# Forty products of a zero block ahead of TensorE's first transposes, an early load of ScalarE's tables, and a new order of the first loads

## The chip, the cores and the metric

The kernel runs on one core of a Trainium2 chip. The metric is the device time of one execution in microseconds (us), as the median of several runs. One more execution was taken by the hardware profiler; its trace gives the rows that are quoted.

## What is computed

Two layers of a transformer trunk for 512 sample tokens and 128 prompt tokens of width 2048, which share all weights. Everything is float32. Cut to what matters:

```python
for layer in range(2):
    sh_p, sc_p, gt_p = modulation(c_ctx, ada_w[layer], ada_b[layer])   # silu(cond) @ ada_w + ada_b
    sh_s, sc_s, gt_s = modulation(c, ada_w[layer], ada_b[layer])       # ada_w[layer]: 2048 x 6144
    hp = rms_norm(xp, norm_g[layer]) * (1.0 + sc_p) + sh_p
    hs = rms_norm(xs, norm_g[layer]) * (1.0 + sc_s) + sh_s
    if layer % 2 == 0:
        out_p, (kc, vc) = even_mixer(hp, *w)      # h @ ev_w_in, banded attention and gated conv, @ ev_w_out
        out_s, _ = even_mixer(hs, *w, ctx=..., rope=rope)
    else:
        out_p, (ckc, cvc, dkc, dvc) = odd_mixer(hp, *w)
        out_s, _ = odd_mixer(hs, *w, ctx=..., rope=rope)
    xp = xp + gt_p * out_p
    xs = xs + gt_s * out_s
```

## The kernel before, in words

Activations stand transposed: a tile `h{k}` holds 128 of the 2048 features (k from 0 to 15) for all 640 tokens, as a high and a low part (`hi`, `lo`). A weight block of 128 x 128 is split in the same way (`wh` by ScalarE, `wl` by VectorE, lines 227 and 228), and a product is three matmuls (`wh` by `hi`, `wh` by `lo`, `wl` by `hi`) for each half of 320 tokens, in the banks `pa`, `pb` or the two halves of `Sp`. The engines' order is made by a scheduler when the program is built; each engine then takes its instructions strictly in that order.

The change touches the **start**. It runs so:

1. SP, ScalarE's queue and GpSimd's queue load the identity, the conditions `c` and `c_ctx` and other short rows (into `rows_a` and `rows_b`, lines 104 to 115) and the tokens, in ten pieces of 512 KB (`xb`, line 101; five blocks of 128 tokens, two halves each).
2. ScalarE and VectorE make silu of the conditions (lines 122 and 123); TensorE transposes the result, and VectorE writes it to `sT` (lines 126 and 127).
3. `x_block` (lines 945 to 960) transposes each token block on TensorE in four groups of four (line 951); VectorE copies three of the groups and ScalarE one (line 952). A group is held in one of two `psT` banks. ScalarE also squares the block (line 956).
4. `ada_on_pe` (lines 173 to 190) multiplies `sT` by tiles of `ada_w` (line 180, "T<-ada,sT" in the profile), which gives scale and shift of a few features at a time. SP loads these tiles by `ada_load` (line 169), 1 MB each, into four buffers that are taken in turn. From unit 1 on, a round of four tiles gives two features: two tiles the scale, two the shift.
5. `lead_units` (lines 331 to 387) works through the features: unit 0 takes features 0 and 1 one after the other (lines 351 to 353), each further unit takes two features (lines 263 to 265). In every unit eight column blocks of the weights are multiplied; for six of them the result is added to a `sum` tile (lines 383 and 385). While unit u runs, the modulation of unit u + 1 is worked out (`ahead`, which calls `ada_group`), and its weights are loaded (`load_two`, line 328, tag `raw`, 4 buffers of 256 KB, two loads each).

Before the change `rows_a`, `rows_b` and `th` are tiles of the tag `raw` too, so three of the four weight buffers are first taken by short rows. Each load counts on one of eight landing semaphores, which the loads of SP's and ScalarE's queue use in turn (DMAHW0 to DMAHW7 in the rows further down): a load of these queues waits until the eighth load before it has landed.

Of the kernel before, what the change touches and what calls it, by code (L numbers as in the profile page):

```python
# [11 lines left out]
F32 = mybir.dt.float32  # L12
F32R = mybir.dt.float32r
BF16 = mybir.dt.bfloat16
AF = mybir.ActivationFunctionType
# [5 lines left out]
P = 128  # L21
# [23 lines left out]
RAW_AHEAD = 5  # L45
SPLIT_AHEAD = 3
FILL0 = 1.68


@with_exitstack  # L50
def trunk_kernel(ctx: ExitStack, tc: tile.TileContext, I: dict, O: dict):
    nc = tc.nc
    V, A, PE, G = nc.vector, nc.scalar, nc.tensor, nc.gpsimd
# [3 lines left out]
    wpool = ctx.enter_context(tc.tile_pool(name="w", bufs=W_BUFS))  # L57
# [6 lines left out]
    def psT():  # L64
        return pT.tile([P, 512], F32, tag="T", name="T")

    def load_rows(dst, name):
        nc.sync.dma_start(dst, I[name][0].partition_broadcast(P))
# [23 lines left out]
    vec = const.tile([P, 160], F32, name="vec")  # L92
    open_pool("start")
    sp = pre = pools["cur"]
    rows_a = wpool.tile([P, P], F32, tag="raw", name="rows_a")
    def x_load(b):
        src = I["x_sample"][0, b * P:(b + 1) * P, :] if b < 4 else I["x_prompt"][0]
        ts = []
        for g in range(2):
            ts.append(hpool.tile([P, 1024], F32, tag=f"h{15 - 2 * b - g}", name="xb"))  # L100
            (nc.scalar if b < 2 else nc.sync).dma_start(ts[g], src[:, g * 1024:(g + 1) * 1024])
        return ts

    nc.sync.dma_start(ident, I["k_ident"])
# [2 lines left out]
    nc.gpsimd.dma_start(rows_a[32:64, :], I["norm_g"].rearrange("l (k p) -> (l k) p", p=P))  # L107
    nc.gpsimd.dma_start(rows_a[64:112, :], I["ada_b"][0].rearrange("(k p) -> k p", p=P))
    xs = [x_load(b) for b in range(5)]
    rows_b = wpool.tile([P, P], F32, tag="raw", name="rows_b")  # L110
    nc.gpsimd.dma_start(rows_b[0:48, :], I["ada_b"][1].rearrange("(k p) -> k p", p=P))
    nc.gpsimd.dma_start(rows_b[48:72, :], I["b_conv"][0].rearrange("t (k p) -> (t k) p", p=P))
    nc.gpsimd.dma_start(rows_b[72:74, :], I["c_out_norm"].rearrange("b (k p) -> (b k) p", p=P))
    for i, n in enumerate(("a_q_norm", "c_q_norm", "d_q_norm")):
        nc.gpsimd.dma_start(rows_b[74 + i:75 + i, :], I[n])

    ada_t = [pre.tile([P, 2048], F32, name=f"ada{i}") for i in range(4)]
    ada_sb = pre.tile([P, 512], F32, name="ada_sb")
    h_t = [pre.tile([P, NT], F32, name=f"ht{i}") for i in range(2)]

    th = wpool.tile([32, P], F32, tag="raw", name="th")
    A.activation(th, rows_a[0:32, :], AF.Tanh, scale=0.5)
    V.scalar_tensor_tensor(out=rows_a[0:32, :], in0=th, scalar=1.0, in1=rows_a[0:32, :],
                           op0=ALU.add, op1=ALU.mult)
# [40 lines left out]
    def ada_load(l, cb, kt, b0, n):  # L165
        m = 16 // n
        w = ada_t[0].rearrange("p (k n) -> p k n", k=m)
        ada_t.append(ada_t.pop(0))
        nc.sync.dma_start(w, I["ada_w"][l, kt * P:(kt + m) * P, cb * 512 + b0 * P:cb * 512 + (b0 + n) * P]
                          .rearrange("(k p) n -> p k n", p=P))  # L170
        return w

    def ada_on_pe(l, cb, b0, n, ws=None):

        acc, m, wd = psT(), 16 // n, n * P
        for kt in range(KT):
            if kt % m == 0:
                w = ws[kt // m] if ws else ada_load(l, cb, kt, b0, n)
            g = kt % 4
            PE.matmul(acc[32 * g:32 * g + 32, 0:wd], sT[:, kt, :], w[:, kt % m, :],  # L180
                      start=(kt < 4), stop=(kt >= KT - 4), tile_position=(0, 32 * g))
        sb = ada_sb
        A.copy(sb[:, 0:wd], acc[:, 0:wd])
        tr = psT()
        for j in range(n):
            PE.transpose(tr[:, j * P:(j + 1) * P], sb[:, j * P:(j + 1) * P], ident)
        red = small.tile([P, n, 2], F32, tag="red", name="red", bufs=2)
        V.tensor_reduce(red, tr[:, 0:wd].rearrange("p (b g c) -> p b c g", b=n, g=4)[:, :, 0:2, :], axis=AX.X,
                        op=ALU.add)
        add_bias(l, cb, red, b0, n)  # L190
        ada_done(l, cb, b0, n)
# [703 lines left out]
    band = const.tile([P, 3, P], BF16, name="band")  # L895
# [4 lines left out]
    gain_rows = const.tile([P, 3, P], F32, name="gain_rows")  # L900
    gains = {n: vec[:, 154 + i:155 + i] for i, n in enumerate(("a_q_norm", "c_q_norm", "d_q_norm"))}
    gains.update({n: gain_rows[:, i, :] for i, n in enumerate(("a_k_norm", "c_k_norm", "d_k_norm"))})
    sink = const.tile([P, 8], F32, name="sink")
# [65 lines left out]
    def ada_group(g, js):  # L969
        for cb in (4 + g, g):  # L970
            ada_on_pe(0, cb, js[0], js[1] - js[0])
        if g == 3 and js[1] == 4:
            for i, n in enumerate(("a_k_norm", "c_k_norm", "d_k_norm")):
                load_rows(gain_rows[:, i, :], n)
            nc.sync.dma_start(band, I["k_band"])
            load_rows(sink, "a_sink")

    def first_loads(cols):

        scale = [ada_load(0, 4, 0, 0, 1)]  # L980
        raws = [load_two(I["ev_w_in"][0], cols[0:2], 0)]
        shift = [ada_load(0, 0, 0, 0, 1)]
        raws += [load_two(I["ev_w_in"][0], cols[i:i + 2], 0) for i in (2, 4, 6)]
        x_block(0, xs[0])
        vec_rows(0, 80, rows_a, 32)
        for b in range(1, 5):
            x_block(b, xs[b])
        last_act[0] = put[0]
        ada_on_pe(0, 4, 0, 1, scale)
        x_rows((0, 1, 2, 3))  # L990
        x_rows((4,))
        vec_rows(80, 77, rows_b, 0)
        ada_on_pe(0, 0, 0, 1, shift)
        return raws
# [143 lines left out]
    for i in range(5, 8):  # L1138
        b_tiles(i)

    u0, c0, b0, h0, g0, g1 = jobs[4:10]
    jobs[0:10] = [u0, c0, jobs[0], jobs[1], g0, jobs[2], jobs[3], g1, b0, h0]
    raws = first_loads([jobs[n][0] for n in (0, 2, 1, 3, 4, 5, 6, 7)])
    run_tiles(jobs, I["ev_w_in"][0], h0_maker, fill0, FILL0, ada_group, trans=TRANS, grace=GRACE, cut=((0, 2), (2, 4)),
              summed=keep, led=even_start, freed=ada_start, first=raws)
    drain(prep)
# [643 lines left out]
```

## Time and profile before

| | |
|---|---|
| median of 3 runs | 2289.78 us (2287.35 to 2291.44) |
| the profiled execution, own time | 2292.61 us |
| its span, first to last instruction | 2290.8 us |
| TensorE busy (matmul) | 2257.0 us, 99% |
| VectorE busy | 1603.5 us, 70% |
| ScalarE busy | 1087.0 us, 47% |
| chain that ended last, share of TensorE | 87% |
| chain that ended last, share of DMA | 3% |

The times in the profile's rows count from the first instruction of the span; 1.8 us of the execution's own time lie around the span. In a row of the timeline stand the start, the time taken, the engine, the line and the instruction; in square brackets how long the engine sat idle before it and what ended that. "SPq" and "ACTq" are instructions that issue a DMA: their duration holds the wait for a free place. One product of float32 operands is two rows of the trace on TensorE ("x10" for five products), a transpose is one. Busy times of TensorE overlap, so a group's cost is read from start to start.

### The profile page before, as it was taken

The page shows a single profiled execution, that of the slowest core. Times are in us where ns is not written, and L with a number is a line of the kernel's source. Part 1 is how long each engine was busy: PE and PEld are TensorE (multiplying, and loading weights), DVE is VectorE, ACT ScalarE, POOL GpSimd, SP SyncE. Part 2 cuts the span into 40 slices and gives each one's busy share as a digit, 9 for nine tenths or more (in the row PEclk, how much of TensorE's full clock was granted, in tenths as well). Part 3 has the DMA queues.
Part 4 walks back from the last instruction along what each step waited for, and adds up shares of the span by engine and source line. Part 5 has one row for each costly group of instructions (what it writes and reads, how often), then busy time and mean ns, then how long its engine had stood idle before and what let it go on. Part 6 is the DMA issues. An engine that isn't in the chain of part 4 may idle for free.

```text
span 2290.8 us, 41085 instructions
## 1 busy us (share of the span) xinstructions
PE 2257.0 (99%) x15941; PEld 2178.5 (95%) x15941; DVE 1603.5 (70%) x2830; ACT 1087.0 (47%) x2281; POOL 162.6 (7%) x226
## 2 busy tenths in 40 slices
PE   7999999999999999999999999999999999999999
PEld 5889999999999999999999999999999999999999
DVE  5666969779779776787787666566566655557775
ACT  5224544244352222544464444465565676654443
POOL 1001000000000000000100001111111100000101
PEclk9999999999999999999999999999999999999999
DMA  9975555555538564854553333423213221238542
GB/s 322 318 224 182 172 155 171 182 153 169 183 107 255 171 190 135 275 168 147 163 157 106 116 118 115 142 61 104 86 56 102 71 65 58 65 109 271 167 137 62
DMA packets 385395, 344.20 MB, mean 150 GB/s; under 512 B 16418, under 2 KB 342528, under 8 KB 384688
## 3 DMA queue, kind: packets, MB, share of 16 engines
q1 hardware_dynamic: 370624, 296.66, 43.4%
q0 software_dynamic: 13856, 42.76, 5.4%
q8 instruction: 125, 2.05, 0.4%
q10 hardware_dynamic: 720, 2.16, 0.3%
q14 instruction: 70, 0.57, 0.1%
HBM read 301.93 MB, written 39.59 MB: 149 GB/s over the span
## 4 chain that ended last, share of the span: by engine, by line
PE 87%; DVE 5%; ACT 4%; DMA 3%; issue 2%; POOL 0%; SPq 0%; DVEq 0%; POOLq 0%; ACTq 0%
PE pq L597 7%; PE pq L596 7%; PE pq L595 7%; PE pa L263 6%; PE pa L264 6%; PE pa L265 6%; PE pb L264 6%; PE pb L263 5%; PE pb L265 5%; PE pb L278 2%; PE pb L277 2%; PE pa L277 2%; PE pb L279 2%; PE pa L279 2%; PE pa L278 2%; PE T L799 2%
## 5 line engine op out<-in xcount | busy, mean ns | idle before, releaser
L227 ACT ACTIVATE wh<-raw 128x512 fp32r<-128x512 f32 x418 | 263.3, 630 | 553.9 <-PE pb L264 388.0
L228 DVE TENSOR_TENSOR wl<-raw,wh 128x512 fp32r<-128x512 f32 x418 | 287.8, 689 | 200.4 <-ACT wh L227 176.8
L263 PE MATMUL pa<-h,wh 128*128 128x320 f32 x978 | 311.2, 319 | 2.4 <-ACT h L227 2.4
L264 PE MATMUL pa<-h,wh 128*128 128x320 f32 x978 | 306.0, 314 | 3.0 <-DVE h L228 2.2
L265 PE MATMUL pa<-h,wl 128*128 128x320 f32 x978 | 303.9, 311 | 0.0
L264 PE MATMUL pb<-h,wh 128*128 128x320 f32 x978 | 302.7, 310 | 0.0
L265 PE MATMUL pb<-h,wl 128*128 128x320 f32 x978 | 302.4, 309 | 0.0
L263 PE MATMUL pb<-h,wh 128*128 128x320 f32 x978 | 301.9, 309 | 0.0
L205 DVE SCALAR_TENSOR_TENSOR acc<-adaw,sT,acc 128x1024 f32<-128x1024 f32 x240 | 300.2, 1278 | 0.0
L595 PE MATMUL pq<-h,wh 128*128 128x320 f32 x672 | 209.2, 311 | 2.3 <-ACT wh L227 2.3
L597 PE MATMUL pq<-h,wl 128*128 128x320 f32 x672 | 208.4, 310 | 0.1
L596 PE MATMUL pq<-h,wh 128*128 128x320 f32 x672 | 208.1, 310 | 0.0
L263 PEld LDWEIGHTS pa<-h,wh 128*128 128x128 f32 x978 | 184.3, 189 | 16.0 <-issue 9.1
L264 PEld LDWEIGHTS pa<-h,wh 128*128 128x128 f32 x978 | 184.7, 189 | 10.5 <-DVE h L228 4.6
L265 PEld LDWEIGHTS pa<-h,wl 128*128 128x128 f32 x978 | 184.7, 189 | 0.4 <-issue 0.4
L264 PEld LDWEIGHTS pb<-h,wh 128*128 128x128 f32 x978 | 183.6, 188 | 1.0 <-issue 0.8
L263 PEld LDWEIGHTS pb<-h,wh 128*128 128x128 f32 x978 | 183.4, 188 | 0.5 <-DVE sum L385 0.4
L265 PEld LDWEIGHTS pb<-h,wl 128*128 128x128 f32 x978 | 183.6, 188 | 0.0
L597 PE MATMUL pq<-T,wl 128*128 128x320 f32 x504 | 155.1, 308 | 0.2 <-DVE wl L228 0.2
L596 PE MATMUL pq<-T,wh 128*128 128x320 f32 x504 | 155.3, 308 | 0.0
L595 PE MATMUL pq<-T,wh 128*128 128x320 f32 x504 | 155.0, 308 | 0.1
L277 PE MATMUL pa<-h,wh 128*128 128x320 f32 x448 | 146.0, 326 | 0.0
(463 smaller groups left out, 5414.1 us busy)
## 6 DMA issues: line engine op xcount, KB each, us to landing
adaw<-in_ada_w SPq DMA_DIRECT2D x128, 512.0 KB, 4.2
raw<-in_ev_w_in SPq DMA_DIRECT2D x176, 256.0 KB, 3.4
raw<-in_od_w_in SPq DMA_DIRECT2D x154, 256.0 KB, 2.9
ada<-in_ada_w SPq DMA_DIRECT2D x32, 1024.0 KB, 9.9
w<-in_od_w_in SPq DMA_DIRECT2D x27, 512.0 KB, 3.9
yd<-y POOLq DMA_DIRECT2D x32, 320.0 KB, 3.6
yin<-yd SPq DMA_DIRECT2D x32, 320.0 KB, 4.5
w<-yd SPq DMA_DIRECT2D x32, 320.0 KB, 4.5
```

The costliest lines, as they stand in the source:

```text
L205: V.scalar_tensor_tensor(out=acc[c], in0=w, scalar=sT[:, kt, c:c + 1], in1=acc[c], op0=ALU.mult, op1=ALU.add)
L227: A.activation(hi, x, AF.Copy)
L228: V.tensor_sub(lo, x, hi)
L263: PE.matmul(ps, wh[:, i, :], hi[:, sl], start=(j == js[0] if alone else (pos == 0 and j == 0)), stop=False)
L264: PE.matmul(ps, wh[:, i, :], lo[:, sl], start=False, stop=False)
L265: last_mm[0] = PE.matmul(ps, wl[:, i, :], hi[:, sl], start=False, stop=(j == js[1] - 1 if alone else (pos == 3 and j == 3)))
L277: PE.matmul(ps, wh[:, j, :], hi[:, sl], start=(qd == 0 and j == 0), stop=False)
L278: PE.matmul(ps, wh[:, j, :], lo[:, sl], start=False, stop=False)
L279: PE.matmul(ps, wl[:, j, :], hi[:, sl], start=False, stop=(qd == 3 and j == 3))
L595: PE.matmul(ps, wh[:, j, :], hi, start=(new and h == 0 and j == 0), stop=False, **kw)
L596: PE.matmul(ps, wh[:, j, :], lo, start=False, stop=False, **kw)
L597: PE.matmul(ps, wl[:, j, :], hi, start=False, stop=(h == 1 and j == 3), **kw)
```

## The change

- A tile `cold` of 128 x 128 is set to zero by VectorE; ScalarE takes the hyperbolic tangent of its first column, ahead of the other work of ScalarE.
- TensorE multiplies `cold` by itself 40 times, into a `psT` bank that nobody reads, ahead of its first transpose.
- The two halves of each sample block are loaded by two queues: the first half by ScalarE's queue, the second by SP's. Before, blocks 0 and 1 were ScalarE's and the others SP's. The prompt block stays with SP.
- `rows_a`, `rows_b` and `th` have places of their own and no longer take buffers of the tag `raw`.
- Four short loads at the end of the modulation are tied behind the last `ada_w` load.

```diff
+WARM = 40
...
     sp = pre = pools["cur"]
-    rows_a = wpool.tile([P, P], F32, tag="raw", name="rows_a")
+    cold = pre.tile([P, P], F32, name="cold")
+    V.memset(cold, 0.0)
+    A.activation(cold[:, 0:1], cold[:, 0:1], AF.Tanh)
+    rows_a = pre.tile([P, P], F32, name="rows_a")
     def x_load(b):
         src = I["x_sample"][0, b * P:(b + 1) * P, :] if b < 4 else I["x_prompt"][0]
         ts = []
         for g in range(2):
             ts.append(hpool.tile([P, 1024], F32, tag=f"h{15 - 2 * b - g}", name="xb"))
-            (nc.scalar if b < 2 else nc.sync).dma_start(ts[g], src[:, g * 1024:(g + 1) * 1024])
+            (nc.sync if b > 3 or g else nc.scalar).dma_start(ts[g], src[:, g * 1024:(g + 1) * 1024])
         return ts
...
-    rows_b = wpool.tile([P, P], F32, tag="raw", name="rows_b")
+    rows_b = pre.tile([P, P], F32, name="rows_b")
...
+    last_ada = [None]
...
+    warm = psT()
+    for _ in range(WARM):
+        PE.matmul(warm[:, 0:P], cold, cold, start=True, stop=True)
+
-    th = wpool.tile([32, P], F32, tag="raw", name="th")
+    th = pre.tile([32, P], F32, name="th")
...
-        nc.sync.dma_start(w, I["ada_w"][l, kt * P:(kt + m) * P, cb * 512 + b0 * P:cb * 512 + (b0 + n) * P]
+        last_ada[0] = nc.sync.dma_start(w, I["ada_w"][l, kt * P:(kt + m) * P, cb * 512 + b0 * P:cb * 512 + (b0 + n) * P]
...
         if g == 3 and js[1] == 4:
-            for i, n in enumerate(("a_k_norm", "c_k_norm", "d_k_norm")):
-                load_rows(gain_rows[:, i, :], n)
-            nc.sync.dma_start(band, I["k_band"])
-            load_rows(sink, "a_sink")
+            with tc.issue_after(last_ada[0].ins):
+                for i, n in enumerate(("a_k_norm", "c_k_norm", "d_k_norm")):
+                    load_rows(gain_rows[:, i, :], n)
+                nc.sync.dma_start(band, I["k_band"])
+                load_rows(sink, "a_sink")
```

The change adds ten lines, so line 180 of the kernel before is line 189 after it, lines 263 to 265 are 272 to 274, and lines 351 to 353 are 360 to 362. Since the scheduler orders the program anew, more moves than the diff shows. Three places matter.

**ScalarE's first instructions.** Before, then after ("cold" is the zero block, "xb" a token half, "th" the hyperbolic tangent of the conditions):

```order
L101 DMA xb<-in_x_sample 128x1024 x4
L122 ACT_TABLE_LOAD
L122 ACTIVATE th<-rows_a 32x128
L956 ACTIVATE sqj,s_224<-xb 128x1024 x2
L956 ACTIVATE sqj,s_260<-xb 128x1024 x2
L952 COPY xT_208<-T 128x4x128
```

```order
L105 DMA xb<-in_x_sample 128x1024
L98 ACT_TABLE_LOAD
L98 ACTIVATE cold<-cold 128x1
L105 DMA xb<-in_x_sample 128x1024 x3
L131 ACTIVATE th<-rows_a 32x128
L965 ACTIVATE sqj,s_268<-xb 128x1024 x2
```

The table load now stands ahead of the activation of the conditions, and three of the four loads on this queue stand behind it. On TensorE the row "L128 MATMUL T<-cold 128x128 x40" stands ahead of everything else.

**SP's queue**, from the last loads of unit 0 to the first tile of the modulation's next round. Before, then after, with the semaphores that each load waits for (`ada_120` to `ada_123` before and `ada_123` to `ada_126` after are the four buffers of `ada_w` tiles):

```order
L169 DMA ada_123<-in_ada_w 128x8x256 [waits DMAHW6_49,DMAHW4_49,PE_49]
L328 DMA raw<-in_ev_w_in 128x2x128 [waits DMASW5_49,DMASW6_49,DMASW4_49,DMASW7_49,DMASW3_49,DMASW2_49]
L328 DMA raw<-in_ev_w_in 128x2x128
L328 DMA raw<-in_ev_w_in 128x2x128 [waits DMAHW7_49,DVE_49]
L328 DMA raw<-in_ev_w_in 128x2x128 [waits DMAHW0_49]
L328 DMA raw<-in_ev_w_in 128x2x128 [waits DMAHW1_49,DVE_49]
L328 DMA raw<-in_ev_w_in 128x2x128 [waits DMAHW2_49]
L328 DMA raw<-in_ev_w_in 128x2x128 [waits DMAHW3_49,DVE_49]
L328 DMA raw<-in_ev_w_in 128x2x128 [waits DMAHW4_49]
L169 DMA ada_120<-in_ada_w 128x8x256 [waits DMAHW5_49,PE_49]
```

```order
L178 DMA ada_125<-in_ada_w 128x8x256 [waits DMAHW7_49,DMAHW4_49,PE_49]
L178 DMA ada_126<-in_ada_w 128x8x256 [waits DMAHW5_49,DMAHW0_49,PE_49]
L337 DMA raw<-in_ev_w_in 128x2x128 [waits DMAHW6_49]
L337 DMA raw<-in_ev_w_in 128x2x128 [waits DVE_49]
L337 DMA raw<-in_ev_w_in 128x2x128
L337 DMA raw<-in_ev_w_in 128x2x128 [waits DMAHW1_49,DVE_49]
L337 DMA raw<-in_ev_w_in 128x2x128 [waits DMAHW2_49]
L337 DMA raw<-in_ev_w_in 128x2x128 [waits DMAHW3_49,DVE_49]
L337 DMA raw<-in_ev_w_in 128x2x128 [waits DMAHW4_49]
L178 DMA ada_123<-in_ada_w 128x8x256 [waits DMAHW5_49,PE_49]
```

Between the last tile of one round and the first tile of the next, eight weight loads stood before and seven stand now; the eighth went ahead of the round's second tile. The place of that first tile in the queue is the same, and so is the set of loads ahead of it. The semaphore it waits for, DMAHW5, belongs to the first of the eight weight loads before, and to the last `ada_w` tile now.

**TensorE at the first product with that tile** (`ada_120` before, `ada_123` now). Before, then after ("h" with a high number are activations of unit 0's second feature or of unit 1):

```order
L263 MATMUL pb<-h_764,wh 128x320
L351 MATMUL pb<-h_609,wh 128x320
L352 MATMUL pb<-h_609,wh 128x320
L353 MATMUL pb<-h_609,wl 128x320
L180 MATMUL T<-ada_120,sT 32x256 x5
L351 MATMUL pa<-h_609,wh 128x320
L352 MATMUL pa<-h_609,wh 128x320
L353 MATMUL pa<-h_609,wl 128x320
L351 MATMUL pb<-h_609,wh 128x320
L352 MATMUL pb<-h_609,wh 128x320
L353 MATMUL pb<-h_609,wl 128x320
L180 MATMUL T<-ada_120,sT 32x256 x3
```

```order
L360 MATMUL pa<-h_653,wh 128x320
L361 MATMUL pa<-h_653,wh 128x320
L362 MATMUL pa<-h_653,wl 128x320
L189 MATMUL T<-ada_123,sT 32x256
L360 MATMUL pb<-h_653,wh 128x320
L361 MATMUL pb<-h_653,wh 128x320
L362 MATMUL pb<-h_653,wl 128x320
L189 MATMUL T<-ada_123,sT 32x256 x4
L360 MATMUL pa<-h_653,wh 128x320
L361 MATMUL pa<-h_653,wh 128x320
L362 MATMUL pa<-h_653,wl 128x320
L360 MATMUL pb<-h_653,wh 128x320
```

Counted from the start of the program, 98 matmuls of 320 tokens stand ahead of the tile's first product before, and 75 now. The 32 products of the round's four tiles stand in five runs before (5, 3, 8, 8 and 8 products) and in nine now (1, 4, 3, 1, 6, 1, 1, 7 and 8); the 32 of the following round stand in three runs before (16, 8 and 8) and in two now (16 and 16). From there on TensorE's order is the same up to small exchanges inside a unit, as is the order of the other engines.

## The prediction

> **What bounds the kernel now.** I read the page first (TensorE busy 99%, 87% of the chain of waits), then that chain by time, for the places where TensorE is not what sets the pace. Near the start, which is all that the change touches, it has these pieces (start, length, what):
>
> ```profile
> 1.67 5.06 DMA rows_a<-in_c_ctx
> 13.60 4.51 PE T L951 x20
> 18.88 0.67 PE T L951 x4
> 24.64 0.67 PE T L951 x4
> 26.08 1.12 PE T L180 x32
> 48.02 8.43 DMA ada<-in_ada_w
> 56.59 1.02 PE T L180 x10
> ```
>
> Until 6.7 us everything waits for a short row. Until 26.08 the token blocks are transposed. Then a chain of small steps leads into unit 0. At 48.02 an `ada_w` tile is issued that lands at 56.45, and TensorE stands still for it. The timeline has TensorE's side of that:
>
> ```profile
> 54.98 0.31 PE L351 MATMUL pb<-h,wh 128*128 128x320 f32 x1
> 56.59 1.02 PE L180 MATMUL T<-ada,sT 128*32 128x256 f32 x10 [1.01 <-DMA ada<-in_ada_w]
> 78.65 1.93 PE L180 MATMUL T<-ada,sT 128*32 128x256 f32 x32
> 97.89 1.86 PE T L180 x32
> ```
>
> So TensorE is released by a landing at 56.45. From there the windows show it busy throughout, and no later piece of the chain up to 190 us is a DMA. What comes after 56.6 us is TensorE's own work, so **the end is the landing of that tile plus the TensorE work that stands behind it**. The landing in turn is set by the DMA engines:
>
> ```profile
> 14.00:16.00 2.00, 2.00 (x11) 1.67 (x10) 1.10 (x3) 1.97 (x4) 0.57 (x1) 1.00 1.03 422
> 26.00:28.00 2.00, 1.53 (x36) 1.27 (x37) 0.81 (x3) 1.37 (x3) 0.00 (x0) 1.00 1.15 326
> 44.00:46.00 2.00, 2.00 (x20) 1.07 (x17) 0.81 (x2) 0.41 (x1) 0.00 (x0) 1.00 1.11 344
> 48.00:50.00 2.00, 2.00 (x27) 1.39 (x20) 1.74 (x4) 0.86 (x2) 0.00 (x0) 1.00 0.71 184
> 70.00:72.00 2.00, 2.00 (x15) 1.85 (x14) 1.97 (x4) 1.83 (x4) 0.00 (x0) 1.00 1.06 353
> ```
>
> The last three columns are granted clock, DMA share and GB/s. The share is over 1 from 8 us to 48 us; only around 49 us it drops. The loads ahead of the tile are as fast as they can be, whatever the engines do.
>
> **The change part by part.**
>
> *The forty products.* The nearest rows are five products of the same form at full speed, and transposes, slow and fast:
>
> ```profile
> 0.95 0.48 DVE L91 MEMSET sT<- 128x512 f32 x1
> 27.71 1.29 PE L966 MATMUL T<-ident,rx 128*128 128x128 f32 x10
> L951 PE MATMUL T<-ident,xb 128*128 128x128 f32 x11 | 2.8, 431 | 0.3 <-DVE vec L132 0.3
> L951 PE MATMUL T<-ident,xb 128*128 128x128 f32 x13 | 2.2, 285 | 0.2
> ```
>
> The last two are the windows 14 to 16 and 18 to 20 us: a transpose goes from 431 to 285 ns, and the chain's 20 from 13.60 give 4.51 / 20 = 0.226 us each while slow. The granted-clock column says 1.00 in both, so I go by the durations. A product is two rows, 2 x 1.29 / 10 = 0.26 us fast with the tail, some 0.23 in a long run, and twice a slow transpose, 0.45, slow. The zero block is ready after VectorE's 1.43 and about 0.2 for a quarter of that memset; I start at 1.8. Forty products end between 1.8 + 40 x 0.23 = 11.0 (never slow) and 1.8 + 40 x 0.45 = 19.8 (never fast). In the trace TensorE became fast near 17.6, 8.8 us after its first work at 8.77 and 4.0 us after its last pause at 13.60. With 4.0 us slow (9 products, 31 fast) the end is 12.9; with 8.8 us (20 and 20) it is 15.2. The products run without pause, so I take 13.5.
>
> The Trainium skill, "TensorE: Matmul & The Clock Gate" (The HAM clock gate), has the default clock halved and released after one busy window of about 3.4 us, which runs free of the kernel; by it the release comes 3.4 to 6.8 us after the start and the products end at an estimated 12.7 to 14.4. The trace agrees with its halving: 0.226 us a transpose against 0.11 us a row fast.
>
> *The transposes behind them.* The first one moves from 8.77 to 13.5. At full speed a group costs half of (24.64 - 18.88) / 4 = 1.44, so 0.72; that is VectorE's copy and the refill of one of two banks, not TensorE:
>
> ```profile
> 18.14 2.13 DVE L952 COPY xT<-T 128x512 f32<-128x512 f32 x3 [0.54 <-PE T L951]
> 23.90 0.70 DVE xT L952
> 12.49 1.03 ACT L956 ACTIVATE sqj<-xb 128x1024 f32<-128x1024 f32 x1 [0.68 <-DMA xb<-in_x_sample]
> 6.80 1.28 ACT L122 ACT_TABLE_LOAD   x1 [6.80 <-DMA rows_a<-in_c_ctx]
> ```
>
> Twenty groups are 14.4, the two row transposes and their copies 1.2, and ScalarE's copy of block 1 stands behind three of its squares, some 0.6: 13.5 + 16.2 = 29.7, where the trace has 26.08. The start of unit 0 comes **3.6 us later** (2.9 to 5.3 for the two ends above). The early table load saves its 1.28 us only on the path to the first transpose, which now waits for the products: nothing.
>
> *The halves and the short rows.* Up to 48 us the DMA engines are full before and after, with the same bytes ahead of the tile but for one weight load of 128 KB. Where SP no longer waits for a short row's buffer, the load only stands longer in a full queue. Nothing, if the engines stay full; behind a start 3.6 us later the refill of an `ada_w` buffer comes 3.6 later, and the queue holds some 3 us of work there.
>
> The Trainium skill, "DMA: Bandwidth & Descriptors" (Issuing engines are not separate DMA queues), says the same of the halves: all queues share 16 engines, and a second issuer saves issue time alone. No price of the sum rests on it.
>
> *The landing.* The tile is issued right after the last weight load before it. That one waited for the previous round's last tile, and the tile itself now waits for it:
>
> ```profile
> L169 SPq DMA_DIRECT2D ada<-in_ada_w x1: 2459/2459/2459, 35.5 to 35.5; - x1
> DMA to landing us min/median/max: 12.0/12.0/12.0
> 38.22 9.70 SPq L328 DMA_DIRECT2D raw<-in_ev_w_in  x8
> 48.02 8.42 SPq L169 DMA_DIRECT2D ada<-in_ada_w  x4
> ```
>
> 35.5 + 12.0 = 47.5, plus 0.35 for 128 KB at 344 GB/s, and the tile is issued at 47.9 to 48.4 against 48.02. Its 8.43 us to landing can shrink by the drop around 49 us, at most (344 - 184) / 344 x 2 = 0.9; it can grow by a late buffer, 0.6. I take 56.3 instead of 56.45: **-0.15**.
>
> *TensorE's work behind the landing.* This is the term that decides. TensorE takes its instructions in order, so it stands at the tile's first product whatever is ready behind it. Now 75 matmuls of 320 tokens are ahead of that place, before 98. Before, the 75th had started by 52.0; now it is reached at 52.0 + 3.6 = 55.6, still ahead of 56.3. So 23 matmuls that ran while the tile was on its way run after it. Their price, and that of a run of `ada_w` products put between them:
>
> ```profile
> 38.74 0.31 PE L353 MATMUL pb<-h,wl 128*128 128x320 f32 x1
> 38.98 0.62 PE L180 MATMUL T<-ada,sT 128*32 128x256 f32 x2
> 39.78 0.31 PE L352 MATMUL pa<-h,wh 128*128 128x320 f32 x1
> 61.47 0.31 PE L265 MATMUL pb<-h,wl 128*128 128x320 f32 x1
> 62.96 0.31 PE L264 MATMUL pa<-h,wh 128*128 128x320 f32 x1
> 64.97 0.31 PE L265 MATMUL pa<-h,wl 128*128 128x320 f32 x1
> 66.72 0.31 PE L265 MATMUL Sp<-h,wl 128*128 128x320 f32 x1
> 61.78 1.00 PE T L180 x16
> ```
>
> From 64.97 to 66.72 are 12 steps: 0.146 us each, so 23 x 0.146 = 3.36. One product between two matmuls takes 39.78 - 38.74 - 2 x 0.146 = 0.75 of its own, eight take 62.96 - 61.47 - 0.29 = 1.20, sixteen 1.20 + 1.86 - 1.00 = 2.06. Up to four cost what one costs (four column groups work at once), five to eight what eight cost. Before: 5, 3, 8, 8, 8, then 16, 8, 8: 4.8 + 0.75 + 2.06 + 2.4 = 10.0. Now: six short runs, three of 6, 7 and 8, then 16, 16: 4.5 + 3.6 + 4.1 = 12.2. **2.2 more.** The other three tiles land 2.9 us apart and are met later than they land.
>
> The sum: 3.36 + 2.2 - 0.15 = +5.4 on a span of 2290.8, so 2296.2. The profiled execution took 2292.61, 2.83 above the median; against the median it is 2289.78 + 5.4 = **2295.2**. Its own range is 2293.8 (landing 0.9 earlier, a short run 0.1 cheaper) to 2297.8 (start 5.3 later: unit 0 reaches the tile at 57.3, 1.0 after the landing; or a landing 0.6 late).
>
> **The rivals.** *The start gains and the wait goes.* If the products end near 11, transposes and first products run at full speed, SP's early weight loads bring the tile earlier, and the 23 matmuls find other idle time in the round, so that only the 1.0 us stall at 56.59 goes and up to 0.9 of the drop: 2289.78 - 1.9 = 2287.9. For it speaks that the stall at 56.59 is real; against it that TensorE has no idle time from 57 to 97 to take 23 matmuls, and that the tile's bytes cannot come sooner.
>
> *Zeros do not wake the clock.* Then all 40 products take 0.45 and end at 19.8, unit 0 starts 9.9 later, and the `ada_w` buffers are freed so late that the DMA queue runs dry: the tile is met at 61.9 instead of 56.59, +5.3 on top of +5.6: 2300.7. For it speaks that nothing in this trace multiplies zeros; against, that the transposes' change of speed came with the time that TensorE had been at work.
>
> *The new order costs nothing*, since VectorE or ScalarE, not TensorE, paces units 1 and 2: then only the landing counts, 2289.6. Against it: VectorE is busy 1.97 of 2 us at 70, but TensorE never waits there.
>
> **How the numbers follow.** The forecast 0.62, the first rival 0.12, the zeros 0.10, the free order 0.16. What this kernel's measurement can tell from no change is about 0.2%, 4.6 us: slower is above 2294.4. The forecast's range lies for four fifths above that, the zeros wholly: 0.62 x 0.8 + 0.10 = 0.60 slower. The rest of the forecast, the free order and half of the first rival are within, 0.34; faster, should the first rival's gain in the round be larger than the stall alone, is 0.06. The range from 2287.5 to 2300.0 takes in the forecast's own range with 2 us more for what the short runs may cost, the free order and most of the first rival, and leaves out the zeros.
>
> **What will show it.** In the changed profile: products from about 1.8 to 12.9 to 15.2, the first `ada_w` product (line 189) near 29.7, the tile's issue near 48 and its landing near 56.3, and TensorE at its first product with an idle time of 0.5 to 1 us; then the run of 32 rows that stood at 78.65 near 84. If that run stands at 79 or before, the term of 23 matmuls is wrong; if TensorE reaches the tile after 57, the products are mis-sized.

## The result, and the profile after

The changed kernel takes 2294.79 us (median of 8 runs, 2293.15 to 2296.82), the kernel before 2287.83 us (8 runs, 2283.78 to 2291.44). The ratio is 1.0025, with a 95% interval from 1.0017 to 1.0034: 5.7 us slower (0.0025 x 2288), between 3.9 and 7.8. The ratios here and below leave out one execution of e3 and three of the kernel before that took over 10% longer than the others.

In the two traces the difference is made in the first 90 us. To follow it through the experiments, this text uses one instruction as a **mark**: the first product of `acc` and `ones` (line 212 before, 221 after), at 325.69 us in the trace of before. The timeline of the changed kernel, TensorE's rows (start, time taken, engine, line, instruction, idle time before and its end):

```profile
2.74 11.83 PE L128 MATMUL T<-cold 128*128 128x128 f32 x80 [2.74 <-ACT cold L98]
14.50 0.24 PE L135 MATMUL T<-ident,rows_a 32*128 32x32 f32 x1
...
29.72 1.08 PE L189 MATMUL T<-ada,sT 128*32 128x128 f32 x32
...
36.37 0.56 PE L360 MATMUL pa<-h,wh 128*128 128x320 f32 x2 [0.20 <-ACT h L1014]
...
55.41 0.30 PE L362 MATMUL pa<-h,wl 128*128 128x320 f32 x1
55.65 0.62 PE L189 MATMUL T<-ada,sT 128*32 128x256 f32 x2
...
83.56 1.93 PE L189 MATMUL T<-ada,sT 128*32 128x256 f32 x32
...
330.59 0.64 PE L221 MATMUL T<-acc,ones 128*32 128x256 f32 x8
```

The products end at 14.5, the first `ada_w` product starts at 29.72 (26.08 before), unit 0 at 36.37 (32.73 before): 3.64 later. The run of 32 rows that stood at 78.65 stands at 83.56, and the mark at 330.59, both 4.9 later. One thing is missing: the row at 55.65, TensorE's first product with the tile, has no idle time in brackets. TensorE came, and the tile was there. The DMA view of that tile, issued at 48.8:

```profile
L178 SPq DMA_DIRECT2D ada<-in_ada_w x1: 368/368/368, 48.8 to 48.8; - x1
...
DMA to landing us min/median/max: 5.4/5.4/5.4
```

48.8 + 5.4 = 54.2 is 1.4 us ahead of TensorE. In the trace of before the same tile took 8.43 us.

The two profiled executions differ by only 1.0 us in their own times (2293.63 against 2292.61) while the mark differs by 4.9: the first execution of before lost time far behind the mark, as the second trace of the same kernel (e4) shows below.

### The profile page after: what moved, and what is told of

Same layout as the page of the kernel before. It is cut to its first block, busy times and chain, and to the rows that moved or that the text cites. A ratio compares the mean times of both kernels' runs of the same rounds, so it can differ in the third digit from the quotient of the medians.

```text
span 2291.9 us, 41258 instructions
## 1 busy us (share of the span) xinstructions
PE 2265.5 (99%) x16021; PEld 2186.4 (95%) x16021; DVE 1603.1 (70%) x2831; ACT 1086.8 (47%) x2282; POOL 162.2 (7%) x226
## 4 chain that ended last, share of the span: by engine, by line
PE 45%; issue 4%; ACT 3%; DVE 3%; DMA 2%; POOL 0%; SPq 0%; POOLq 0%; DVEq 0%; ACTq 0%
PE pq L606 7%; PE pq L605 7%; PE pq L604 7%; PE pa L286 2%; PE pb L287 2%; PE pb L286 2%; PE pb L288 2%; PE pa L288 2%; PE pa L287 2%; PE T L633 1%; PE T L808 1%; PE S L820 1%; PE S L822 1%; PE S L821 1%; ACT qsw L708 1%
```

## The experiments

Each run has a trace. The table gives, for all of them, where unit 0 starts (first product of `h` and `wh`), how far the mark is from there, TensorE's waits of over 0.3 us for a landing or an activation up to 60 us (summed), and the mark. Further on, near 210 and 240 us, every trace has the same two waits (0.6 to 0.8 and 0.7 us), and three have one more of 0.3. "Order" is that of TensorE at the tile: 98 matmuls of 320 tokens ahead of its first product as before, or 75 with the short runs of the change. Times with an interval are ratios to the kernel before; the runs without a time are one execution each, too few to tell differences of this size.

| run | order | unit 0 | to the mark | waits in it | mark | time |
|---|---|---|---|---|---|---|
| before, first trace | before | 32.73 | 292.96 | 1.01 | 325.69 | 1 |
| before, second trace (e4) | before | 32.22 | 292.44 | 0.89 | 324.66 | |
| halves alone (e6) | before | 33.05 | 291.56 | none | 324.61 | |
| short rows alone (e7) | before | 32.78 | 292.54 | 0.94 | 325.32 | |
| halves and rows (e11) | before | 32.91 | 292.35 | 0.42 | 325.26 | |
| early table load alone (e10) | before | 33.90 | 291.70 | none | 325.60 | |
| the change, no products (e1) | before | 33.87 | 292.99 | 1.02 | 326.86 | 1.0003 (0.9994 to 1.0012) |
| forty products, late tile (e3) | 98 ahead, fewer runs | 35.72 | 291.41 | none | 327.13 | 1.0013 (1.0004 to 1.0022) |
| the change, first trace | change | 36.37 | 294.22 | none | 330.59 | 1.0025 (1.0017 to 1.0034) |
| the change, second trace (e9) | change | 36.51 | 294.23 | none | 330.74 | |
| before, early tile (e5) | 78 ahead | 32.69 | 293.92 | 1.95 | 326.61 | 1.0005 (0.9996 to 1.0013) |
| sixteen products alone (e8) | before | 32.13 | 293.71 | none, but half clock | 325.84 | 1.0008 (0.9999 to 1.0017) |
| the change, sixteen (e2) | before | 34.70 | 293.97 | none, but half clock | 328.67 | 1.0006 (0.9997 to 1.0015) |

### No products (e1)

```diff
-WARM = 40
+WARM = 0
```

> The whole change but for the forty products (none are issued). The mark for all runs is the first product of acc and ones, far behind the start: it starts at 325.69 us in the trace of before and at 330.59 in that of the change. TensorE's order at the tile is that of before again (98 matmuls of 320 tokens ahead of the tile's first product). If the products alone make the change slow: the first ada_w product near 26 (25 to 27.5), the tile lands near 56.4 as before, mark 324.7 to 326.5, time within 0.2% of before. If the new order of the token halves (the second half of block 0 landed at 10.88 in the change's trace, 6.37 before) or the short rows cost something by themselves: first ada_w product after 27.5, mark above 327.

Measured: first `ada_w` product at 26.76, mark 326.86, ratio 1.0003 (0.9994 to 1.0012). TensorE's rows:

```profile
26.76 1.08 PE L189 MATMUL T<-ada,sT 128*32 128x128 f32 x32 [0.18 <-DVE xT L961]
...
32.86 1.08 PE L189 MATMUL T<-ada,sT 128*32 128x128 f32 x32 [0.67 <-DMA ada<-in_ada_w]
...
36.44 0.82 PE L189 MATMUL T<-ada,sT 128*32 128x128 f32 x21 [1.02 <-DMA ada<-in_ada_w]
...
326.86 0.64 PE L221 MATMUL T<-acc,ones 128*32 128x256 f32 x8
```

Without the products the time cannot be told from before, so they, with the order that they bring, are what is measured. The mark is 3.7 us ahead of the change's but still 1.2 behind before's, a little beyond the first theory's band and short of the second's: TensorE waits 0.67 and 1.02 us for the third and fourth `ada_w` tile. The tile landed at 54.24, not near 56.4 as expected. The tiles that come late here led to e6, e7, e10 and e11.

### Sixteen products, with the change's loads and alone (e2, e8)

```diff
-WARM = 40
+WARM = 16
```

> Sixteen products of the zero block in place of forty, all else as in the change. In the change's trace 13 products are slow (0.43 us each, 2.74 to 8.2) and the others 0.224: sixteen end near 8.9, and the transposes run at full speed from there; the second half of block 0 lands near 10.9, so the first ada_w product starts near 24.3, 1.8 before that of before. TensorE's order at the tile is that of before. Theory A, the end is the tile's landing and the work behind it: landing near 56.2, TensorE waits some 2.4 us there, mark 325.5, time as before. Theory B, the shift of the start goes through to the end because the tile lands earlier than TensorE reaches it: no wait, mark 322.9, time 2.8 us below before.

In e8 the kernel before has the zero block, its memset and sixteen products, and nothing else of the change:

```diff
+    cold = pre.tile([P, P], F32, name="cold")
+    V.memset(cold, 0.0)
...
+    warm = psT()
+    for _ in range(16):
+        PE.matmul(warm[:, 0:P], cold, cold, start=True, stop=True)
```

> The kernel before with sixteen products of the zero block, which wait for VectorE's memset alone (no early hyperbolic tangent), and the loads of before. Products from about 1.8, slow for 4 to 5.5 us, end before 9; transposes at full speed from 9.0, the first ada_w product near 23.5 where before has 26.08 and 25.04. If the start goes through: mark near 323.2 and time 2.5 us below before. If the landings of the ada_w tiles are the floor: TensorE waits some 2 to 3 us for tiles between 30 and 36, mark 324.0 to 325.0, time as before within 0.1%.

In both, the products did what they can do: the transposes ran at full speed from the start. The first `ada_w` product came at 24.39 in e8, earlier than in both traces of before (26.08 and 25.04), and at 25.38 in e2, where the tokens land late. In neither was it worth anything: marks 325.84 and 328.67, times 0.08% and 0.06% above before with intervals that hold no change. TensorE's rows of e2, then the windows of e2 over the same time (the column ahead of the last two is the granted clock):

```profile
32.83 1.93 PE L189 MATMUL T<-ada,sT 128*32 128x128 f32 x32 [2.02 <-DMA ada<-in_ada_w]
...
34.70 0.90 PE L360 MATMUL pa<-h,wh 128*128 128x320 f32 x2
```

```profile
28.00:30.00 2.00, 1.55 (x36) 1.05 (x34) 1.16 (x3) 0.76 (x2) 0.00 (x0) 1.00 1.12 323
30.00:32.00 2.00, 0.37 (x5) 0.14 (x1) 0.33 (x2) 1.02 (x3) 0.00 (x0) 0.93 1.16 295
...
34.00:36.00 2.00, 2.00 (x21) 1.62 (x14) 0.00 (x0) 0.27 (x1) 0.00 (x0) 0.50 1.12 321
```

TensorE waits 2.02 us for the third tile, and the clock that the products had won is taken back, to 0.50 from 31.7 to 38.5 us. In e8 the wait is 1.29 us, and the clock is at half for 3.4 us from 32.2 (TensorE's rows, then that window):

```profile
31.12 1.08 PE L186 MATMUL T<-ada,sT 128*32 128x128 f32 x32 [1.29 <-DMA ada<-in_ada_w]
...
32.13 0.83 PE L357 MATMUL pa<-h,wh 128*128 128x320 f32 x2
```

```profile
32.20:35.60 3.40, 3.40 (x30) 2.95 (x33) 1.12 (x5) 1.65 (x4) 0.00 (x0) 0.51 1.13 345
```

Both expectations named the landings as one case, and in kind that case held: the earlier first product ended in a longer wait. The numbers missed. In e2 the wait was expected at the tile near 56 us with the mark at 325.5, and it came at the third tile; in e8 the first `ada_w` product was expected near 23.5, the waits at 2 to 3 us and the mark at 324.0 to 325.0. That the wait would also go with a loss of the clock was not foreseen. That loss is the larger part of e2's delay: e1, with the same landings of the third and fourth tile within 0.1 us (32.7 and 36.3) and the full clock, has its mark 1.2 us behind before's first trace, and e2 3.0.

### Forty products with before's order (e3)

```diff
+        u0_mm = []
...
                 last_mm[0] = PE.matmul(ps, wl[:, j, :], hi[:, sl], start=False, stop=alone)
+                u0_mm.append(last_mm[0])
...
-                        ahead(*units[ui + 1][1:])
+                        with tc.issue_after(u0_mm[29].ins) if ui == 1 else ExitStack():
+                            ahead(*units[ui + 1][1:])
```

> The change with forty products, but with the tile's products tied behind a matmul of unit 0, so that 98 matmuls of 320 tokens stand ahead of the first again, and the 64 products of the two rounds stand in runs of 5, 3, 1, 7, 16, 16 and 16. TensorE did not wait at the tile in the change, so its place by itself costs nothing there and only the shorter runs do: mark 330.59 - 2.3 = 328.3, time 2.3 us below the change. If splitting the products into short runs costs nothing: mark 330.6. If the 23 matmuls behind the landing were the price (3.4) on top of the runs: mark 325.0.

Measured: mark 327.13, ratio 1.0013 (1.0004 to 1.0022). TensorE's `ada_w` products from the tile on, in e3 (with unit 0's start) and then in the change (each row is one run of products, x2 being one product; the x8 at 60.53 is the runs of 3 and 1, which touch). The change's next run is the one at 83.56 shown above:

```profile
35.72 0.56 PE L361 MATMUL pa<-h,wh 128*128 128x320 f32 x2 [0.20 <-ACT h L1017]
...
58.48 1.05 PE L189 MATMUL T<-ada,sT 128*32 128x256 f32 x10
...
60.53 0.64 PE L189 MATMUL T<-ada,sT 128*32 128x256 f32 x8
...
63.05 1.06 PE L189 MATMUL T<-ada,sT 128*32 128x256 f32 x14
...
65.05 1.93 PE L189 MATMUL T<-ada,sT 128*32 128x256 f32 x32
...
80.12 1.94 PE L189 MATMUL T<-ada,sT 128*32 128x256 f32 x32
```

```profile
55.65 0.62 PE L189 MATMUL T<-ada,sT 128*32 128x256 f32 x2
...
56.84 0.64 PE L189 MATMUL T<-ada,sT 128*32 128x256 f32 x8
...
58.48 0.63 PE L189 MATMUL T<-ada,sT 128*32 128x256 f32 x6
...
59.82 0.62 PE L189 MATMUL T<-ada,sT 128*32 128x256 f32 x2
...
61.44 1.06 PE L189 MATMUL T<-ada,sT 128*32 128x256 f32 x12
...
63.08 0.62 PE L189 MATMUL T<-ada,sT 128*32 128x256 f32 x2
...
64.62 0.62 PE L189 MATMUL T<-ada,sT 128*32 128x256 f32 x2
...
67.12 1.06 PE L189 MATMUL T<-ada,sT 128*32 128x256 f32 x14
...
68.76 1.07 PE L189 MATMUL T<-ada,sT 128*32 128x256 f32 x16
```

From unit 0's start to the run of 32 rows TensorE needs 80.12 - 35.72 = 44.40 us in e3 and 83.56 - 36.37 = 47.19 in the change, with the same 205 matmuls of 320 tokens between. The 2.8 us are the short runs: between 59.82 and 61.44 stand one product and six matmuls, 1.62 - 6 x 0.146 = 0.74 for a single product, and the run of sixteen at 65.05 in e3 takes 1.93 for all of them. The mark came 1.2 earlier than expected: unit 0 started 0.65 earlier (the clock was granted earlier, and the products ended at 13.8, not 14.5; see the end), and the short runs cost 2.8 rather than 2.3. Against e1, with the same loads, the same place of the tile and no products, forty products shift unit 0 by 1.85 and the mark by only 0.27: 1.0 of the difference is the wait that e1 has, and the other 0.6 goes with e3's order, whose runs (5, 4, 7, 16, 16 and 16) are longer than e1's. So **most of what the products cost comes from the order that the scheduler makes because of them**: of the 3.7 us between e1 and the change it is 2.8 by e3, and 2.2 by the distance from unit 0 to the mark in e1 itself (294.22 - 292.99 + 1.02). The times go the same way, 1.0003, 1.0013 and 1.0025, with intervals that overlap from one to the next. The order is not all of it: e3 stays 0.13% above before, with its mark 1.4 and 2.5 us behind before's two.

### Before, once more, and the change once more (e4, e9)

> The kernel before once more, for a second trace of the same program. The mark within 0.2 us of 325.69. In the comparison of the first two traces the change's lead over before falls from 4.9 us (160 to 900 us) to 3.4 near 970 and to 1.0 near 2120. If that is one execution against another, this trace differs from the first of the same kernel by as much in those places; if it belongs to the change, it agrees with the first within 0.3 us up to the end.

The mark is 324.66, 1.03 earlier than in the first trace, not within 0.2. TensorE's rows, then the tile's DMA (issued at 47.9):

```profile
31.20 1.08 PE L180 MATMUL T<-ada,sT 128*32 128x128 f32 x32 [0.73 <-DMA ada<-in_ada_w]
...
34.64 1.08 PE L180 MATMUL T<-ada,sT 128*32 128x128 f32 x32 [0.89 <-DMA ada<-in_ada_w]
...
55.73 0.64 PE L180 MATMUL T<-ada,sT 128*32 128x256 f32 x8
...
324.66 0.64 PE L212 MATMUL T<-acc,ones 128*32 128x256 f32 x8
```

```profile
L169 SPq DMA_DIRECT2D ada<-in_ada_w x1: 421/421/421, 47.9 to 47.9; - x1
...
DMA to landing us min/median/max: 5.9/5.9/5.9
```

The stall at the tile, on which the prediction was built, is not there: the tile was issued at the same moment and landed at 53.80, not 56.45. Other tiles, at 31 and 35, are waited for instead. The rest of the expectation is answered too: from the mark to the end this trace takes 2284.1 - 324.66 = 1959.4 us, the first one 2290.8 - 325.69 = 1965.1, and the two of the change 1961.3 and 1960.1. In the nine other traces it is 1958.3 to 1962.6. The 4 us by which the change's first trace seemed to catch up belong to the first execution of before.

> The changed kernel once more, for a second trace of the same program. In its first trace unit 0 starts at 36.37, TensorE reaches the tile at 55.65, 1.4 after its landing, and the mark comes 294.22 us after unit 0's start, where six traces with the order of before show 291.4 to 292.0 beside their waits. If the order is what costs: the distance from unit 0's start to the mark is 294.2 again, plus any wait at the tile. If it was that execution: 291.4 to 292. The products' end moves with the moment at which TensorE becomes fast (8.28 in the first trace of the change, 6.67 in the run of forty products with the other order): 13.8 to 14.5, unit 0's start 35.7 to 36.4, mark 329.9 to 330.6.

Unit 0's start to the mark is 294.23 us (294.22 in the first trace), with no wait, as expected if the order is what costs; the products ended at 13.5 and the mark is 330.74, 0.1 to 0.3 us outside what was expected of them:

```profile
2.74 10.78 PE L128 MATMUL T<-cold 128*128 128x128 f32 x80 [2.74 <-ACT cold L98]
...
36.51 0.56 PE L360 MATMUL pa<-h,wh 128*128 128x320 f32 x2 [0.20 <-ACT h L1014]
...
55.80 0.62 PE L189 MATMUL T<-ada,sT 128*32 128x256 f32 x2
...
330.74 0.64 PE L221 MATMUL T<-acc,ones 128*32 128x256 f32 x8
```

So the order costs the same in both executions. Unit 0 starts no earlier although the products ended 1.0 earlier: the chain of waits goes here through a token half that lands at 14.0.

```profile
2.58 11.41 DMA xb<-in_x_sample
```

### The tile's place alone (e5)

The kernel before, with the products of the round's four tiles moved up on TensorE and the rest of unit 0 tied behind the first of them; the loads keep their order.

```diff
+                    if ui == 0 and c == 1 and i == 3:
+                        gate_mm[0] = None
+                        ahead(*units[2][1:])
...
                     if ui == 0:
-                        one_block(ui, c, n, part, pp)
+                        with tc.issue_after(gate_mm[0].ins) if (c == 1 and i >= 3) else ExitStack():
+                            one_block(ui, c, n, part, pp)
```

> The kernel before, with the products of the round's four tiles forced to an earlier place on TensorE: 78 matmuls of 320 tokens ahead of the tile's first product (98 before, 75 in the change); the 64 products of the two rounds stand in runs of 8, 8, 8, 8, 16 and 16. SP's queue is that of before. It tests the term of the prediction by itself: matmuls put behind the landing are paid in full. TensorE comes to the tile near 52.4 (51.3 if the start is 1.0 earlier, as in the second trace of before); the tile lands between 53.8 and 56.5, as in the two traces of before. If the place counts: TensorE waits there by the difference, 1.4 to 4.1 us, and the mark is 325.7 plus that wait, less the 1.0 of the old one, less 1.1 for the longer runs: 325.0 to 327.7 (326.5 in the middle), time 0 to 2 us above before. If the place costs nothing, since VectorE or ScalarE paces the units behind it: 324.6 or less with any wait at the tile.

```profile
50.93 0.30 PE L356 MATMUL pb<-h,wl 128*128 128x320 f32 x1
...
52.37 0.41 PE L266 MATMUL pa<-h,wh 128*128 128x320 f32 x1 [1.13 <-ACT h L1013]
...
54.86 1.07 PE L181 MATMUL T<-ada,sT 128*32 128x256 f32 x16
...
326.61 0.64 PE L215 MATMUL T<-acc,ones 128*32 128x256 f32 x8
```

The mark, 326.61, lies where the first theory put it (325.0 to 327.7), but not by a wait at the tile: some matmuls of unit 1 stand ahead of the tile in this order, and TensorE waits 1.13 us for unit 1's activations; it comes to the tile at 54.86, after its landing at 54.12. With the matmuls of unit 0 put behind, there was nothing ready to run in their place. So the place is paid for here, by 1.13 us and smaller gaps, and the experiment does not show the price of a wait for the landing, since none came about.

### The loads, part by part (e6, e7, e11, e10)

e6 and e7 each make one edit of the change to the kernel before; e11 is the change without its products and without the early hyperbolic tangent, and so has both edits, the zero block's memset and the short loads tied behind the last `ada_w` load.

```diff
-            (nc.scalar if b < 2 else nc.sync).dma_start(ts[g], src[:, g * 1024:(g + 1) * 1024])
+            (nc.sync if b > 3 or g else nc.scalar).dma_start(ts[g], src[:, g * 1024:(g + 1) * 1024])
```

> The kernel before, with the two halves of each sample block on two queues as in the change, and nothing else. The last token half landed at 17.5 and 17.6 us in the two traces of before and at 18.4 to 19.2 in the four traces with the whole change of loads; the third ada_w tile at 30.2 and 31.1 against 31.8 to 32.7. If the halves are the reason: last half near 18.4, third tile near 32, mark 326 to 327. If not: 17.5, 30 to 31, mark 324.6 to 325.7.

```diff
-    rows_a = wpool.tile([P, P], F32, tag="raw", name="rows_a")
+    rows_a = pre.tile([P, P], F32, name="rows_a")
...
-    rows_b = wpool.tile([P, P], F32, tag="raw", name="rows_b")
+    rows_b = pre.tile([P, P], F32, name="rows_b")
...
-    th = wpool.tile([32, P], F32, tag="raw", name="th")
+    th = pre.tile([32, P], F32, name="th")
```

> The kernel before, with places of their own for the three tiles of short rows, and nothing else. By the prediction's step it costs and gains nothing: last token half near 17.5, third ada_w tile at 30 to 31, mark 324.6 to 325.7. If the weight loads that no longer wait for the short rows' buffers take bytes from the tokens: last half near 18.4, mark above 326.

> The change without its products and without the early hyperbolic tangent: halves on two queues and own places for the short rows, together. If these two make the loads late only together: last token half near 18.4 and mark 326 to 327. If the early table load is the reason: 17.5 and mark 324.6 to 325.7.

The last token half landed at 17.58, 17.58 and 17.17; the marks are 324.61, 325.32 and 325.26. The third `ada_w` tile landed at 30.2, 31.6 (expected 30 to 31) and 30.6; in the two traces of before it was 30.2 and 31.1. Neither edit costs or gains anything at the mark that these traces show.

e10 is the kernel before with the early table load:

```diff
+    cold = pre.tile([P, P], F32, name="cold")
+    V.memset(cold, 0.0)
+    A.activation(cold[:, 0:1], cold[:, 0:1], AF.Tanh)
```

> The kernel before with the zero block, its memset and the early hyperbolic tangent, and nothing else: no products, the loads of before. ScalarE's table load then stands between the first token load of its queue and the other three. In the four traces with the whole change of loads the last token half landed at 18.4 to 19.2, in the four of before or with halves or rows alone at 17.5 to 17.6. If the table load's place is the reason: 18.4 here, third ada_w tile near 32.5, mark 326 to 327. If not: 17.5, TensorE's first work near 7.5 in place of 8.8, mark 324.6 to 325.7.

ScalarE's rows in e10, then its last token half in the DMA view (L104, issued at 10.9), then the same of before (L101):

```profile
0.74 0.41 ACTq L104 DMA_DIRECT2D xb<-in_x_sample  x1
1.19 1.28 ACT L97 ACT_TABLE_LOAD   x1 [1.19 <-PEq L1780]
1.62 0.86 ACTq L104 DMA_DIRECT2D xb<-in_x_sample  x2
```

```profile
L104 SPq DMA_DIRECT2D xb<-in_x_prompt x1: 328/328/328, 10.9 to 10.9; - x1
...
DMA to landing us min/median/max: 7.8/7.8/7.8
```

```profile
L101 SPq DMA_DIRECT2D xb<-in_x_prompt x1: 328/328/328, 10.3 to 10.3; - x1
...
DMA to landing us min/median/max: 7.3/7.3/7.3
```

10.9 + 7.8 = 18.7 against 10.3 + 7.3 = 17.6: with the early table load alone the tokens come 1.1 us late, as in all five traces that have it with the change's loads (18.4 to 19.2), and as in none without it (17.2 to 17.8). The first `ada_w` product comes 1.2 us later (27.25), although TensorE's first work came 2.2 us earlier (6.61). The third `ada_w` tile lands at 31.4 (expected near 32.5 if the table load is the reason). The mark is 325.60, level with before's first trace (325.69) and 0.9 behind its second: with before's order a start 1.2 us late mostly disappears in the waits for tiles, of which e10 has none. e1, which has the table load and the other edits together, has its mark 1.3 to 1.6 us behind those of e10 and e11; no run here shows why. Why the table load slows the loads was not tried; its place between the token loads' issues is what the rows show, and the issues on ScalarE's queue moved by 0.4 us at most.

## Why the prediction was right

The forecast was 5.4 us slower; the measured ratio says 5.7 (3.9 to 7.8), and the mark, taken over two traces of each kernel, says 330.67 - 325.18 = 5.5. The sum is right in size, but the case that the forecast describes, TensorE held at the tile and then paying for 23 matmuls, did not happen: its largest term stands for something else, and that the total came out is partly luck.

- **The products' end and unit 0's start: right.** Expected 13.5 (11.0 to 19.8) and 3.6 us later; measured 14.5 and 13.5, and 3.64. Two errors nearly cancel in the first trace. The products did not start at 1.8 after VectorE's memset but at 2.74, since ScalarE's hyperbolic tangent writes a column of the block they read, and so they wait for the table load that the prediction had counted as free (the row's releaser is "ACT cold L98"; in e8, without it, they start at 1.63). From the products' end to the first `ada_w` product it took 15.2 us instead of 16.2. In the second trace the late start is made up by an earlier full clock, and the transposes take 16.3 us behind it.
- **Halves and rows: nothing, right** for the mark, each by itself and together (e6, e7, e11). **The early table load: wrong,** it makes the tokens 1 us late (e10). Before's order hides that; in the changed kernel it is covered by the products for the most part.
- **The landing of the tile: wrong, and this is the step that failed.** The prediction took 8.43 us from issue to landing from one execution and allowed 0.9 less. The same tile, issued between 47.9 and 49.3, took 5.4 to 8.4 us in the traces here, 5.9 in the second one of before. In the changed kernel it landed at 54.2, and TensorE came at 55.65 and did not wait. The bytes show where the time went: between issue and landing of this tile of 1.05 MB, the engines moved 294 GB/s x 8.43 us = 2.5 MB in the first trace of before, 279 x 5.87 = 1.6 MB in the second and 296 x 5.42 = 1.6 MB in the change. The loads ahead of the tile had landed by 50.8 and 50.6 us in the two traces of before, so in the first some 0.8 MB more of the tiles issued behind it went through beside it. The Trainium skill, "DMA: Bandwidth & Descriptors" (Two DMAs through the same engine are not ordered), says that nothing orders transfers across the 16 engines, and the trace agrees with that. What makes it more in one execution than in another was not tried.
- **The 23 matmuls behind the landing (3.36 us): right in size by chance.** With no wait at the tile, their place by itself costs nothing in this kernel; what goes through is the start's own delay, less the wait that before had. Over two traces of each: unit 0 starts 36.44 - 32.48 = 3.96 later, less 0.95 us of waits, so 3.0, where the prediction had 3.36 - 0.15 = 3.2. The two accounts meet where TensorE comes just as the tile lands, and the prediction had it come only 0.7 us ahead (55.6 and 56.3).
- **The short runs (2.2 us): right, somewhat small.** The distance from unit 0's start to the mark, waits taken out, is 294.2 with the change's order and 291.4 to 292.0 in the eight traces with 98 matmuls ahead and the full clock: 2.2 to 2.8. e3, where the products stand behind 98 matmuls again and in fewer runs, is 2.8 us shorter than the change.
- **The range's upper end (2297.8)** does not follow from the two cases given for it. A start that reaches the tile 1.0 after the landing adds 1.0 to 2295.2, and a landing 0.6 late adds at most 0.75, so neither gives more than 2296.2.
- **The rivals.** Zeros do wake the clock (it was granted 3.3 to 5.5 us after the first product in the five runs that have products). An early start does not gain: in e2 and e8 it was bought and lost again at the third tile. The order is not free, by e3.

No timed version here beats the kernel before: e1, e2, e3, e5 and e8 are 0.03% to 0.13% above it, with marks from 325.8 to 328.7. Where the start was made earlier (e2, e8), it was the landing of the third `ada_w` tile that held it.

## What to carry to other kernels

Instructions that warm an engine up gained nothing here, since loads paced the start: a faster start waited longer at the next load. Where a scheduler orders the program, ask what it does with added work, since here the runs that it cut into pieces cost 2.2 to 2.8 of 5.5 us. A transfer's time from one execution is one draw: before a sum is built on one landing, take a second trace, and work the sum out for both sides of the wait.

## What the runs showed of the hardware beyond that

- The moment at which TensorE becomes fast moves from run to run of the same program. In the two traces of before the recorded full clock begins at 17.5 and 13.4 us, in the two of the change at 8.3 and 6.1, with the first product at 2.74 in both: 5.5 and 3.4 us of slow work. The Trainium skill, "TensorE: Matmul & The Clock Gate" (The HAM clock gate), has a window of some 3.4 us that runs free of the kernel, and the traces agree with that. In the five runs with products it took 3.3 to 5.5 us: the clock came at the end of a stretch of 3.41 us that the products had filled to 97% or more (in e8 3.30 us from 1.52 to 4.93; in the change 3.41 us from 4.87 to 8.28, after 2.13 us in the stretch before, which brought nothing).
- The clock was taken back after short waits in a thin stretch. In e8 TensorE waited 1.29 us, after 27 us at full clock (from 4.9) and in a stretch of small steps (0.88 us busy of the two from 30 to 32), and had 0.50 for the next 3.4 us. In the second trace of before, waits of 0.73 and 0.89 at nearly the same places cost no clock, nor did 0.67 and 1.02 in e1. What tells them apart in the first 60 us of all 13 traces is TensorE's busy time in a stretch of 3.41 us at full clock, counted from where the record of the full clock begins. The clock was at half behind the three such stretches with the least: 1.68 us in e8 (28.83 to 32.24), 1.62 in e2 (28.30 to 31.71) and 0.38 in e10 (12.31 to 15.72). It stayed full behind all others, of which the least is 1.87 (12.92 to 16.33 in the second trace of the change). This count is not the whole rule: near 1130 us the clock was also lost behind stretches busy for 74% to 80%.
